# One Trainium2 core, a whole network: the seam between the two halves of its attention, and the routing of its experts, rearranged

## The chip, the cores and the metric

The kernel runs on one core of one Trainium2 chip. A core has five engines that run side by side, each from a queue of its own in fixed order: TensorE (PE) for matrix products, VectorE (DVE), ScalarE (ACT), GpSimd (POOL) and SyncE (SP), which mostly starts DMA transfers. They wait for each other through semaphores. The metric is the device time of one execution in microseconds; lower is better.

## The reference, cut to what matters

The reference is a chain of blocks over 512 tokens of width 1024: differential attention, a mixture of 16 experts, and then two layers of other mixers and feed-forward blocks. The change touches the first block and the routing of the second:

```
def diff_attention(x, w_in, ...):        # H = 8 heads, dh = 64
    q, k, v = split(x @ w_in)            # q, k: H x 2 x dh, normed over dh; v: H x 128
    for s in range(0, T, 128):           # 4 query blocks of 128, causal
        sc = q[s:s+128] . k[:s+128] - slope * distance
        p  = softmax(sc);  pd = p[first] - lam * p[second]
        outs.append(pd @ v[:s+128])
    return rmsnorm(concat(outs)) * (1 - lam0) @ w_out

def hier_moe(x, ...):                    # 4 groups of 4 experts
    logit_g = x @ w_group + b_group;   g_sel = argmax(logit_g)
    logit_e = (x @ w_router + b_router)[g_sel]
    top_v, top_i = top_k(softmax(logit_e), 2)
    # every token is computed by its two experts, weighted by top_v and the group's gate
```

## The kernel before

**Products.** Every large product is made three times with split operands (high part by high part, high by low, low by high): lines 139 to 141 where the tokens are the stationary side, 135 to 137 where the weights are. A weight block of 128x1024 numbers is split by a ScalarE cast (`wh`, L110) and a VectorE subtraction (`wl`, L111), so each block of weights costs both engines a step ahead of the products that read it (24 in a projection).

**Attention** is `stage_a`. Its eight heads are two halves, `G` = 0 and 1. `project(G)` makes q, k and v of a half: 48 units, 16 for each of q, k and v, each unit six products of 128x512. `headnorm` norms q and k per head: a VectorE sum (L445), the twelve small VectorE steps of `rsq` (L286 to L293), a scaling (L451), four TensorE transposes (L458) and a ScalarE copy (L459).

`attend(G)` is a list of 20 units. A unit holds the score products of a query block `i` and head `hh` (L487, two of them into the two banks named `s`), the transposes of an earlier head's probabilities (L505, into the only bank named `t`; ScalarE copies them out at L507), and the value products of a still earlier one (L514). Between the products VectorE adds the distances to the scores (L488) and mixes the two softmax parts (L494 to L497), and ScalarE takes the exponentials (L491). After the fourth head of a query block `onorm` norms the output (sum L526, `rsq`, scaling L530) and `turn_o` transposes it (L539) into the tiles `oh` and `ol`, which the output products `out(G)` read (8 units of 12 products, L135 to L137). For `i` = 0 a score product is 128x128, for `i` = 1 it is 128x256, then 384 and 512.

**Order.** `emit` writes units out in a given order, and `after(us, fn)` puts a step off by a number of units' cost. `weave(a, b)` merges two lists by the middle of each unit's cost, so that the units of the shorter list are spread evenly along the other; `tail=4` keeps the last four units of `b` for the end. The program before emits `project(0)`; then `attend(0)` woven with all 48 units of `project(1)`; then `attend(1)` woven with `out(0)`; then `out(1)`, whose results go through `route_step`.

**Routing.** For each of eight chunks `route_step` adds the residual (L378), squares it on ScalarE (L273) and adds the squares on GpSimd (L277), multiplies with the router's weights into the bank `lp` (L1171), transposes the chunk (L1177) and stores it to the buffer `xn` by a DMA that SP issues (L1180). `norm_r` sums the squares over partitions with eight products against ones (`ss`, L351), and `rsq` turns them into `rt`. `route` makes the logits `lg`, finds the best and the second expert in each group by two calls of `first_max`, forms the one-hot masks `M1`, `M2` and their sum `Mb`, and counts each token's place in its expert's list by products with a triangular matrix (`rk`, L1230). `rm` is that place (L1240, L1242). `places` compares it to a row of numbers (`oh`, L1300) and gets each expert's token numbers by products (`tk`, L1301) into `gix`. GpSimd then gathers those rows of `xn` into a tile `xe` (an indirect DMA, L1342), which has been cleared (L1322) because an expert's list is rarely full. `prep` transposes `xe` (L1353), and the first expert's products begin. `weigh` makes the tokens' weights, which GpSimd splits in three (L1288, L1291) for four small products each (`tkb`).

Of the kernel before, what the change touches and what calls it, by code (L numbers as in the profile page):

```python
# [29 lines left out]
def _constants():  # L30
# [26 lines left out]
    put("before", (p < j).astype(np.float32))  # L57
    put("iota", j)
    put("tokhi", np.broadcast_to((np.arange(NT)[:, None] * 128.0 - SKIP), (NT, 16)).reshape(1, -1))
# [22 lines left out]
class K:  # L82
# [261 lines left out]

    def norm_r(self, want_b=True, now=False):

        nc = self.nc
        ss = self.ptt("ss")
        for n, sq in enumerate((self.acc, self.acc2)):
            for i in range(NT):  # L350
                nc.tensor.matmul(ss[:, i:i + 1], lhsT=sq[:, i * P:(i + 1) * P], rhs=self.ones, start=n + i == 0, stop=n == 1,  # L351
                                 skip_group_check=True)
        self.rt = self.rsq(ss[:, :NT], NT, 1.0 / D, name="rt")
# [37 lines left out]
    def stage_a(self):  # L391
# [3 lines left out]
        with tc.tile_pool(name="pa", bufs=1) as pa:  # L395
# [76 lines left out]
            def attend(G):  # L472
                q, k, v = qkv[G]
                pvs, pt, p2s = {}, {}, {}

                def begin():
                    o[G] = (self.x8("oh"), self.x8("ol"))

                def score(i, hh):
# [40 lines left out]
                def onorm(i, pv):  # L520
# [12 lines left out]

                    def turn_o():
                        oh, ol = o[G]
                        qs = slice(i * P, i * P + P)
                        tp = self.ptt()
                        for hh in range(4):
                            nc.tensor.transpose(tp[:, hh * P:(hh + 1) * P], s[:, hh * P:(hh + 1) * P], self.ident)  # L539
                        tv = tp.rearrange("p (a b) -> p a b", a=4)  # L540
                        nc.scalar.activation(oh[:, :, qs], tv, AF.Copy, scale=gs[:, 1:2])
                        nc.vector.scalar_tensor_tensor(ol[:, :, qs], tv, gs[:, 1:2], oh[:, :, qs].bitcast(F32),
                                                       op0=OP.mult, op1=OP.subtract)
# [5 lines left out]
                for t in range(len(us) + ATT[1]):  # L549
# [8 lines left out]

                    def fn(parts=parts, t=t):
                        if t == 0:  # L560
                            begin()
                        for f, u, _ in parts:
                            f(*u)
# [8 lines left out]
            p1 = project(1)  # L572
            self.emit(self.weave(attend(0), p1))
            self.emit(self.weave(attend(1), out(0, self.add_h), tail=4))
            self.flush()
# [545 lines left out]
    def moe_begin(self, pool):  # L1121
# [14 lines left out]
        nc.scalar.dma_start(f, a["cst"][:, o:o + 388])  # L1136
        self.four = pr.tile([P, 4], F32, name="four")
        nc.gpsimd.tensor_copy(self.four, f[:, 0:4])
        nc.gpsimd.tensor_copy(self.before, f[:, 4:132])
# [14 lines left out]
    def route_step(self, pool):  # L1154
# [4 lines left out]
        def done(m, ps):  # L1159
# [8 lines left out]

            def turn():
                for i in range(NT):  # L1170
                    nc.tensor.matmul(self.lp[:, i * 20:(i + 1) * 20], lhsT=self.h[:, m, i * P:(i + 1) * P],  # L1171
                                     rhs=self.wrt[:, m], start=m == 0 and i == 0, stop=m == NK - 1, skip_group_check=True)
                if m == NK - 1:
                    self.norm_r(want_b=False)
                tp = self.ptt()
# [9 lines left out]
    def route(self):  # L1185
# [12 lines left out]
        parts(rt[:, :, None].to_broadcast([P, NT, NE]), 3)  # L1198
        fours = self.four[:, None, :].to_broadcast([P, NT * 5, 4])

        def first_max(src, tag):

            mx, eq, vm = (pr.tile([P, NT * 5, n], F32, name=tag + w) for w, n in (("m", 1), ("e", 4), ("v", 1)))
            nc.vector.tensor_reduce(mx, src, axis=AX.X, op=OP.max)
            nc.vector.tensor_tensor(eq, src, mx.to_broadcast([P, NT * 5, 4]), op=OP.is_equal)
            nc.vector.tensor_tensor(eq, eq, fours, op=OP.mult)
            nc.vector.tensor_reduce(vm, eq, axis=AX.X, op=OP.max)
            oh = pr.tile([P, NT, 5, 4], F32, name=tag + "o")
            nc.vector.tensor_tensor(oh.rearrange("p i g e -> p (i g) e"), eq, vm.to_broadcast([P, NT * 5, 4]),
                                    op=OP.is_equal)  # L1210
            return mx, oh


        lg4 = lg.rearrange("p i (g e) -> p (i g) e", e=4)
        mx, oh1 = first_max(lg4, "a")
        goh = oh1[:, :, 0, :, None].to_broadcast([P, NT, 4, 4])
        le2 = pr.tile([P, NT * 5, 4], F32, name="le2")
        nc.vector.scalar_tensor_tensor(le2, oh1.rearrange("p i g e -> p (i g) e"), NEG, lg4, op0=OP.mult, op1=OP.add)
        mx2, oh2 = first_max(le2, "b")
        M = [t3("M1", 4, 4), t3("M2", 4, 4)]  # L1220
# [11 lines left out]
        for j in range(NT):  # L1232
# [8 lines left out]
                                       op1=OP.mult)  # L1241
        nc.vector.tensor_scalar(rm, rm, -1.0, None, op0=OP.add)  # L1242

# [16 lines left out]
        def weigh():  # L1260

            lge, ges, dm, e2, w = t3("lge", 4), t3("ges", 1), t3("dm", 4), t3("e2", 1), t3("w", NE)
            mv = lambda t: t.rearrange("p (i g) o -> p i (g o)", g=5)
            nc.vector.tensor_tensor(lge, lg[:, :, 0:4], mv(mx)[:, :, 0:1].to_broadcast([P, NT, 4]), op=OP.subtract)
# [48 lines left out]
    def stage_b(self):  # L1313
# [5 lines left out]
        with tc.tile_pool(name="pb", bufs=1) as pb:  # L1319
            xes = [pb.tile([P, D], F32, name=f"xe{i}", tag=f"xe{i}") for i in range(3)]  # L1320
            for t in xes:
                nc.gpsimd.memset(t, 0.0)  # L1322
            flip = [0, 0]
# [401 lines left out]
```

## Time and profile before

| what | value |
|---|---|
| three timed runs | 1922.05, 1922.75, 1923.62 us |
| median | 1922.75 us |
| the profiled execution | 1921.22 us |
| its span | 1919.5 us |
| mean granted TensorE clock | 0.984 |
| TensorE busy | 1841.3 us, 96% |
| VectorE busy | 1321.3 us, 69% |
| ScalarE busy | 975.1 us |
| GpSimd busy | 227.3 us |

The profile is of one execution. Its span runs from the first instruction to the last; 1.7 us lie around it in that execution's time, which is 1.5 us under the median of the timed runs. The granted clock is 1.00 at 2.4 GHz and 0.50 at 1.2 GHz.

### The profile page before, as it was taken

To read this page: it belongs to the slowest core of one execution; us is meant where nothing else is said; L and a number is where in the kernel's file an instruction comes from. 1 tells how busy PE (TensorE), PEld (TensorE's weight loads), DVE (VectorE), ACT (ScalarE), POOL (GpSimd) and SP (SyncE) were. 2 spreads that over 40 slices of the span, in tenths; PEclk is the share of its full clock that TensorE was granted. 3 is DMA by queue.
4 is the path that set the end of the run, shared out by engine and by line. 5 is a ranking of instruction groups with operands and counts; after the bars stand their busy time and mean duration, and the time that the engine had idled before them with its cause. 6 is when DMAs were issued, how large, how long until landed. Compare 5 with 4: busy or idle time off the path is not lost.

```text
span 1919.5 us, 24632 instructions
## 1 busy us (share of the span) xinstructions
PE 1841.3 (96%) x8604; PEld 1451.1 (76%) x8605; DVE 1321.3 (69%) x2817; ACT 975.1 (51%) x1660; POOL 227.3 (12%) x281
## 2 busy tenths in 40 slices
PE   8999996999998999998999999999999999999997
PEld 6767585778887877675688888887877788888885
DVE  6586757999997779855677447744476677637753
ACT  5565554888885424436554224434276544324442
POOL 2000012222221301310200000012200100000001
PEclk9999897999999999999999999999999999999998
DMA  5521047999995454445233343334545233243331
GB/s 189 180 67 56 33 159 239 345 372 365 370 374 202 123 136 116 113 135 133 68 91 93 86 114 92 86 90 136 140 115 130 57 102 92 83 118 93 85 87 59
DMA packets 260098, 274.74 MB, mean 143 GB/s; under 512 B 14438, under 2 KB 175622, under 8 KB 259968
## 3 DMA queue, kind: packets, MB, share of 16 engines
q1 hardware_dynamic: 250688, 257.56, 43.8%
q0 software_dynamic: 5072, 10.00, 1.5%
q10 hardware_dynamic: 4208, 5.56, 0.8%
q8 instruction: 69, 1.13, 0.2%
q14 instruction: 61, 0.50, 0.1%
HBM read 238.19 MB, written 15.73 MB: 132 GB/s over the span
## 4 chain that ended last, share of the span: by engine, by line
PE 56%; DVE 7%; DMA 2%; ACT 2%; issue 1%; POOL 1%; SPq 0%; DVEq 0%; ACTq 0%; POOLq 0%
PE mm L135 15%; PE mm L137 15%; PE mm L136 15%; PE pv L721 2%; PE t L709 1%; DVE wl L111 1%; DVE sc L884 1%; DVE m L883 1%; PE mm L139 1%; PE mm L140 1%; PE mm L141 1%; PE s L694 1%; PE pv L1095 1%; DVE sb L697 1%; ACT sb L698 0%
## 5 line engine op out<-in xcount | busy, mean ns | idle before, releaser
L110 ACT CAST wh<-wr 128x1024 fp32r<-128x1024 f32 (+5 forms) x335 | 306.7, 916 | 440.6 <-PE mm L136 322.1
L111 DVE TENSOR_TENSOR wl<-wr,wh 128x1024 fp32r<-128x1024 f32 (+4 forms) x332 | 356.2, 1076 | 201.0 <-ACT wh L110 198.3
L135 PE MATMUL mm<-xh,wh 128*128 128x512 f32 x952 | 372.5, 391 | 2.0 <-DVE h L378 1.8
L137 PE MATMUL mm<-xh,wl 128*128 128x512 f32 x952 | 372.2, 391 | 0.2 <-DVE wl L111 0.2
L136 PE MATMUL mm<-xl,wh 128*128 128x512 f32 x952 | 371.3, 390 | 0.0
L135 PEld LDWEIGHTS mm<-xh,wh 128*128 128x128 f32 x952 | 178.8, 188 | 39.7 <-issue 3.5
L137 PEld LDWEIGHTS mm<-xh,wl 128*128 128x128 f32 x952 | 178.8, 188 | 37.9 <-issue 1.1
L136 PEld LDWEIGHTS mm<-xl,wh 128*128 128x128 f32 x952 | 178.8, 188 | 36.3 <-issue 0.2
L111 DVE TENSOR_TENSOR wl<-wx,wh 128x1024 fp32r<-128x1024 f32 x123 | 151.8, 1252 | 11.8 <-ACT wh L110 5.8
L110 ACT CAST wh<-wx 128x1024 fp32r<-128x1024 f32 x134 | 139.5, 1051 | 29.3 <-PE mm L141 24.4
L139 PE MATMUL mm<-wh,xh 128*128 128x512 f32 (+2 forms) x352 | 131.8, 378 | 9.7 <-ACT wh L110 5.6
L135 PE MATMUL mm<-hh,wh 128*128 128x512 f32 x352 | 138.9, 395 | 0.0
L136 PE MATMUL mm<-hl,wh 128*128 128x512 f32 x352 | 138.9, 395 | 0.0
L137 PE MATMUL mm<-hh,wl 128*128 128x512 f32 x352 | 138.9, 395 | 0.0
L140 PE MATMUL mm<-wl,xh 128*128 128x512 f32 (+2 forms) x352 | 130.0, 370 | 3.4 <-DVE wl L111 3.4
L141 PE MATMUL mm<-wh,xl 128*128 128x512 f32 (+2 forms) x352 | 129.0, 367 | 0.0
L618 DVE TENSOR_TENSOR z<-mm,rb 128x512 f32<-128x512 f32 x88 | 60.4, 688 | 81.0 <-PE mm L137 81.0
L139 PE MATMUL mm<-wh,xeh 128*128 128x512 f32 x256 | 103.8, 406 | 0.8 <-ACT xeh L1356 0.8
L277 POOL TENSOR_TENSOR acc<-acc,sq 128x512 f32<-128x512 f32 x42 | 58.1, 1383 | 387.6 <-ACT sq L273 387.2
L141 PE MATMUL mm<-wh,xel 128*128 128x512 f32 x256 | 101.6, 397 | 0.0
L140 PE MATMUL mm<-wl,xeh 128*128 128x512 f32 x256 | 101.2, 395 | 0.0
L378 DVE TENSOR_TENSOR h<-mm,h 128x512 f32<-128x512 f32 x88 | 60.5, 690 | 52.1 <-PE mm L137 50.9
(412 smaller groups left out, 3365.2 us busy)
## 6 DMA issues: line engine op xcount, KB each, us to landing
wr<-in_ffn_w_up SPq DMA_DIRECT2D x88, 512.0 KB, 4.9
wx<-in_moe_w_gate SPq DMA_DIRECT2D x23, 1024.0 KB, 9.4
wx<-in_moe_w_up SPq DMA_DIRECT2D x22, 1024.0 KB, 8.2
wx<-in_moe_w_down SPq DMA_DIRECT2D x22, 1024.0 KB, 9.9
wr<-in_ffn_w_down SPq DMA_DIRECT2D x32, 704.0 KB, 4.6
wr<-in_da_w_in SPq DMA_DIRECT2D x11, 1024.0 KB, 5.2
wr<-in_even_w_in SPq DMA_DIRECT2D x11, 1024.0 KB, 5.6
wr<-in_moe_w_up SPq DMA_DIRECT2D x10, 1024.0 KB, 8.4
```

The source lines that it names most:

```text
L110: nc.scalar.copy(h, raw)
L111: (nc.gpsimd if eng else nc.vector).tensor_tensor(l, raw, h.bitcast(F32), op=OP.subtract)
L135: mm(out, lhsT=wh, rhs=xh, start=first, stop=False, skip_group_check=True)
L136: mm(out, lhsT=wh, rhs=xl, start=False, stop=False, skip_group_check=True)
L137: mm(out, lhsT=wl, rhs=xh, start=False, stop=last, skip_group_check=True)
L139: mm(out, lhsT=xh, rhs=wh, start=first, stop=False, skip_group_check=True)
L140: mm(out, lhsT=xh, rhs=wl, start=False, stop=False, skip_group_check=True)
L141: mm(out, lhsT=xl, rhs=wh, start=False, stop=last, skip_group_check=True)
L277: nc.gpsimd.tensor_tensor(self.acc, self.acc, sq, op=OP.add)
L378: self.nc.vector.tensor_tensor(self.h[:, m], ps, self.h[:, m], op=OP.add)
L618: nc.vector.tensor_tensor(z[:, 2:], ps, self.rb, op=OP.mult)
L721: nc.tensor.matmul(pv[64 * e:64 * e + 64, j * P:], lhsT=heads[u]["v"](j), rhs=pt[:, 4 * j:3 * j + 4], start=j == 0, stop=j == NT - 1, skip ...
```

## The change

There are four edits.

1. `attend(0)` is woven with the first 40 units of `project(1)` only. The first four units of `attend(1)` (the scores of `i` = 0) are woven with the last eight units, which are value products; the other sixteen units of `attend(1)` go with `out(0)` as before. The tiles `oh` and `ol` are taken at the first use.
2. The products that sum the squares are in two parts, and in the routing they use a bank named `s` in place of `t`. The part that reads the running sum comes ahead of the last chunk's logits.
3. The best and second experts come from a comparison of each pair in a group: a logit's place is the number of logits ahead of it. The row of numbers counts from 1, which saves the subtraction of 1 from `rm`. What only the weights need moves into `weigh`.
4. ScalarE clears the three `xe` tiles, in place of GpSimd.

```
-    put("iota", j)
+    put("iota", j + 1)
...
+    def norm_sums(self, ss, n):
+
+        sq = (self.acc, self.acc2)[n]
+        for i in range(NT):
+            self.nc.tensor.matmul(ss[:, i:i + 1], lhsT=sq[:, i * P:(i + 1) * P], rhs=self.ones, start=n + i == 0, stop=n == 1,
+                                  skip_group_check=True)
...
                     def turn_o():
+                        if G not in o:
+                            o[G] = (self.x8("oh"), self.x8("ol"))
                         oh, ol = o[G]
...
             p1 = project(1)
-            self.emit(self.weave(attend(0), p1))
-            self.emit(self.weave(attend(1), out(0, self.add_h), tail=4))
+
+            self.emit(self.weave(attend(0), p1[:-8]))
+            a1 = attend(1)
+            self.emit(self.weave(a1[:4], p1[-8:]))
+            self.emit(self.weave(a1[4:], out(0, self.add_h), tail=4))
...
             def turn():
+                if m == NK - 1:
+                    ss = self.pst("ss")
+                    self.norm_sums(ss, 0)
                 for i in range(NT):
...
                 if m == NK - 1:
-                    self.norm_r(want_b=False)
+                    self.norm_r(want_b=False, ss=ss)
...
-        mx, oh1 = first_max(lg4, "a")
+        vs = pr.tile([P, NT * 5, 4, 4], F32, name="vs")
+        own = lambda j, n: lg4[:, :, j:j + 1].to_broadcast([P, NT * 5, n])
+        nc.vector.tensor_tensor(vs, lg4[:, :, None, :].to_broadcast([P, NT * 5, 4, 4]),
+                                lg4[:, :, :, None].to_broadcast([P, NT * 5, 4, 4]), op=OP.is_gt)
+        for j in range(1, 4):
+            nc.vector.tensor_tensor(vs[:, :, j, 0:j], lg4[:, :, 0:j], own(j, j), op=OP.is_ge)
+        place = pr.tile([P, NT * 5, 4], F32, name="place")
+        nc.vector.tensor_reduce(place, vs, axis=AX.X, op=OP.add)
+        oh1, oh2 = (pr.tile([P, NT, 5, 4], F32, name=n) for n in ("oh1", "oh2"))
+        for n, oh in enumerate((oh1, oh2)):
+            nc.vector.tensor_scalar(oh.rearrange("p i g e -> p (i g) e"), place, float(n), None, op0=OP.is_equal)
...
-        mx2, oh2 = first_max(le2, "b")
...
-        nc.vector.tensor_scalar(rm, rm, -1.0, None, op0=OP.add)
...
-                nc.gpsimd.memset(t, 0.0)
+                nc.scalar.activation(t, self.ones.to_broadcast([P, D]), AF.Copy, scale=0.0)
```

The instructions of each engine stand in one fixed order, before and after. On TensorE, at the end of `project(1)` (products of L139 to L141) and the start of `attend(1)` (`s` scores, `t` transposes, `pv` value products, `mm<-oh,wh` and the like the output products), the rows before are these; the left name is what an instruction writes.

```order
L141 MATMUL mm<-wh,xl_110 128x512
L487 MATMUL s<-kt,qt 128x128 x7
L505 MATMUL t<-ident,p_1962 128x128
L514 MATMUL pv<-v,pt 128x128
L539 MATMUL t<-ident,os 128x128 x4
L487 MATMUL s<-kt,qt 128x128
L487 MATMUL s<-kt,qt 128x256
L135 MATMUL mm<-oh,wh 128x512 x2
```

In the change the same place reads as follows, from one pair of scores to the last projection product and the first output product.

```order
L490 MATMUL s<-kt,qt 128x128 x2
L508 MATMUL t<-ident,p_1982 128x128
L139 MATMUL mm<-wh,xh_108 128x512
L140 MATMUL mm<-wl,xh_108 128x512
L141 MATMUL mm<-wh,xl_110 128x512
L139 MATMUL mm<-wh,xh_108 128x512
L140 MATMUL mm<-wl,xh_108 128x512
L141 MATMUL mm<-wh,xl_110 128x512
L490 MATMUL s<-kt,qt 128x256 x2
L517 MATMUL pv<-v,pt 128x128 x2
...
L135 MATMUL mm<-oh,wh 128x512
```

The four pairs of 128x128 scores have moved among the last 48 projection products (this is the last of the four pairs), and the first 128x256 score stands right behind the last of these products. From the last score of `attend(0)` to the end of the projection there were 66 products and are now 102; the last 42 of them stand among the pairs.

On VectorE, between the logits and the mask `Mb` (`am`, `bm` are the group maxima, `ae` to `ao` and `be` to `bo` the steps of `first_max`), before has these rows among others:

```order
L1196 TENSOR_TENSOR lg<-lg,rows 128x80
L1204 TENSOR_REDUCE am<-lg 128x20
L1205 TENSOR_TENSOR ae<-lg,am 128x80
...
L1209 TENSOR_TENSOR ao<-ae,av 128x80
L1218 SCALAR_TENSOR_TENSOR le_2968<-ao,lg 128x80
...
L1204 TENSOR_REDUCE bm<-le_2968 128x20
...
L1209 TENSOR_TENSOR bo<-be,bv 128x80
...
L1225 TENSOR_TENSOR Mb<-M_2979,M_2980 128x64
```

The change has there:

```order
L1203 TENSOR_TENSOR lg<-lg,rows 128x80
L1210 TENSOR_TENSOR vs<-lg 128x320
L1263 TENSOR_REDUCE mx<-lg 128x20
L1213 TENSOR_TENSOR vs<-lg 128x20
L1213 TENSOR_TENSOR vs<-lg 128x20x2
L1213 TENSOR_TENSOR vs<-lg 128x20x3
L1269 TENSOR_TENSOR lge<-lg,mx 128x16
L1215 TENSOR_REDUCE place<-vs 128x80
L1275 TENSOR_REDUCE ges<-lge 128x4
L1218 TENSOR_SCALAR oh_2964<-place 128x80
L1218 TENSOR_SCALAR oh_2965<-place 128x80
...
L1225 TENSOR_TENSOR Mb<-M_2968,M_2969 128x64
```

From the second `lg` to `Mb` there were 19 instructions between; there are 13.

On ScalarE, behind the last stores' copies (`xk`) and the first exponential of `weigh` (`lge`), the change has these rows, where before the second exponential came next and then two casts:

```order
L1186 COPY xk<-t 128x512 x2
L1273 ACTIVATE lge<-lge 128x16
L1327 ACTIVATE xe_3046<-ones 128x1024
L1327 ACTIVATE xe_3047<-ones 128x1024
L1327 ACTIVATE xe_3048<-ones 128x1024
L110 CAST wh<-wx 128x1024
L1274 ACTIVATE e_3061<-e_3061 128x4
L110 CAST wh<-wx 128x1024
L1361 CAST xeh<-t 128x512 x2
```

The three clears stand ahead of the first cast and of the second exponential, which two small chains (the weights, and the first expert's low parts) wait for.

## Rows read from the trace of the kernel before

**Rows 1.** The page: busy times, and the granted clock in 40 slices.
```profile
PE 1841.3 (96%) x8604; PEld 1451.1 (76%) x8605; DVE 1321.3 (69%) x2817; ACT 975.1 (51%) x1660; POOL 227.3 (12%) x281
...
PEclk9999897999999999999999999999999999999998
```

**Rows 2.** Three stretches: length, busy of PE, PEld, DVE, ACT, POOL, clock, DMA.
```profile
188.66:194.10 5.44, 3.73 (x22) 2.61 (x21) 5.39 (x42) 3.60 (x13) 0.00 (x0) 1.00 0.82 255
194.10:207.00 12.90, 12.90 (x33) 7.37 (x32) 6.56 (x34) 5.56 (x19) 0.00 (x0) 0.50 0.14 56
207.00:211.03 4.03, 3.93 (x18) 2.19 (x18) 2.88 (x18) 2.12 (x7) 0.00 (x0) 0.91 0.00 0
```

**Rows 3.** Timeline of PE: start, duration, instruction, idle before it and its releaser.
```profile
188.12 0.39 PE L140 MATMUL mm<-wl,xh 128*128 128x512 f32 x1
188.34 0.39 PE L141 MATMUL mm<-wh,xl 128*128 128x512 f32 x1
188.66 0.49 PE L487 MATMUL s<-kt,qt 64*128 64x128 f32 x4
189.63 2.24 PE L487 MATMUL s<-kt,qt 64*128 64x128 f32 x10 [0.47 <-DVE st L488]
...
211.03 0.92 PE L487 MATMUL s<-kt,qt 64*128 64x384 f32 x4
```

**Rows 4.** Two stretches of 10 us, columns as in group 2.
```profile
160.00:170.00 10.00, 8.32 (x41) 5.57 (x40) 8.62 (x32) 4.72 (x11) 0.00 (x0) 1.00 0.33 107
...
210.00:220.00 10.00, 9.78 (x44) 5.29 (x43) 8.88 (x50) 6.77 (x21) 0.00 (x0) 1.00 0.00 0
```

**Rows 5.** PE's longest wait between 80 and 188 us.
```profile
PE t L458 <- ACT pt L507: 1.7, 1, 1.7
```

**Rows 6.** Timeline of DVE: first and last row of the k norms' bunch.
```profile
151.56 0.68 DVE L445 TENSOR_REDUCE qss<-sq 128x8 f32<-128x512 f32 x1
...
163.86 1.21 DVE L111 TENSOR_TENSOR wl<-wr,wh 128x1024 fp32r<-128x1024 f32 x1
```

**Rows 7.** Timeline of all engines, routing, 291 to 300 us.
```profile
291.32 1.02 PE L351 MATMUL ss<-ones,acc 128*128 128x1 f32 x8 [0.60 <-ACT xk L1179]
...
295.95 0.24 DVE L1196 TENSOR_TENSOR lg<-lg,rows 128x80 f32<-128x80 f32 x1
...
299.60 0.22 DVE L1225 TENSOR_TENSOR Mb<-M,M 128x64 bf16<-128x64 f32 x1
```

**Rows 8.** Timeline of all engines, routing, 300 to 313 us.
```profile
300.27 1.99 ACT L110 CAST wh<-wx 128x1024 fp32r<-128x1024 f32 x2 [0.92 <-DMA xn<-xk]
...
300.38 2.89 POOL L1322 MEMSET xe<- 128x1024 f32 x3 [2.32 <-DMA xn<-xk]
...
300.53 0.22 DVE L1240 SCALAR_TENSOR_TENSOR rm<-rk,Ms 128x64 f32<-128x64 f32 x1
...
300.79 0.60 DVE L1242 TENSOR_SCALAR rm<-rm 128x64 f32<-128x64 f32 x1
...
301.42 1.98 DVE L1300 TENSOR_SCALAR oh<-iota,rm 128x128 bf16<-128x128 bf16 x6
...
303.84 0.15 DVE L1307 TENSOR_SCALAR gix<-tf 128x1 int32<-128x1 f32 x1
...
304.88 1.25 POOL L1342 DMA_INDIRECT xe<-xn,gix  x1 [1.61 <-DVE w L1279]
...
309.71 0.88 PE L1353 MATMUL t<-ident,xe 128*128 128x128 f32 x3 [5.18 <-DVE ohl L1432]
...
311.28 0.41 DVE L1300 TENSOR_SCALAR oh<-iota,rm 128x128 bf16<-128x128 bf16 x2
...
312.09 0.78 PE L139 MATMUL mm<-wh,xeh 128*128 128x512 f32 x1
```

**Rows 9.** A stretch in the experts' products, columns as in group 2.
```profile
360.00:420.00 60.00, 60.00 (x290) 48.03 (x289) 59.75 (x82) 50.80 (x60) 18.37 (x11) 1.00 1.03 372
```

**Rows 10.** SP's longest waits there and ahead, 314 to 584 us.
```profile
SPq L1333 <- DVE wl L111: 93.6, 42, 4.7
```

More of the change, by code (lines that the diff above doesn't have):

```diff
@@ L343, in new_acc, with norm_r @@
         self.acc = self.sm.tile([P, T], F32, name="acc", tag="sq", bufs=3)
-    def norm_r(self, want_b=True, now=False):
-        nc = self.nc
[L348 to L352, printed above, removed]
+    def norm_sums(self, ss, n):
[3 more added lines that the diff above has]
+                                  skip_group_check=True)
+    def norm_r(self, want_b=True, now=False, ss=None):
+        nc = self.nc
+        if ss is None:
+            ss = self.ptt("ss")
+            self.norm_sums(ss, 0)
+        self.norm_sums(ss, 1)
         self.rt = self.rsq(ss[:, :NT], NT, 1.0 / D, name="rt")
@@ L474, in attend @@
                 pvs, pt, p2s = {}, {}, {}
-                def begin():
-                    o[G] = (self.x8("oh"), self.x8("ol"))
                 def score(i, hh):
@@ L557, in attend, with fn @@
                     cost = sum(c * (u[0] + 1) * 0.45 for _, u, c in parts)
-                    def fn(parts=parts, t=t):
-                        if t == 0:
-                            begin()
+                    def fn(parts=parts):
                         for f, u, _ in parts:
@@ L1136, in moe_begin @@
         nc.scalar.dma_start(f, a["cst"][:, o:o + 388])
-        self.four = pr.tile([P, 4], F32, name="four")
-        nc.gpsimd.tensor_copy(self.four, f[:, 0:4])
         nc.gpsimd.tensor_copy(self.before, f[:, 4:132])
@@ L1169, in turn @@
             def turn():
+                if m == NK - 1:
+                    ss = self.pst("ss")
+                    self.norm_sums(ss, 0)
                 for i in range(NT):
@@ L1198, in route @@
         parts(rt[:, :, None].to_broadcast([P, NT, NE]), 3)
[L1199 to L1211, printed above, removed]
-        lg4 = lg.rearrange("p i (g e) -> p (i g) e", e=4)
-        mx, oh1 = first_max(lg4, "a")
+        lg4 = lg.rearrange("p i (g e) -> p (i g) e", e=4)
+        vs = pr.tile([P, NT * 5, 4, 4], F32, name="vs")
[9 more added lines that the diff above has]
+            nc.vector.tensor_scalar(oh.rearrange("p i g e -> p (i g) e"), place, float(n), None, op0=OP.is_equal)
         goh = oh1[:, :, 0, :, None].to_broadcast([P, NT, 4, 4])
-        le2 = pr.tile([P, NT * 5, 4], F32, name="le2")
-        nc.vector.scalar_tensor_tensor(le2, oh1.rearrange("p i g e -> p (i g) e"), NEG, lg4, op0=OP.mult, op1=OP.add)
-        mx2, oh2 = first_max(le2, "b")
         M = [t3("M1", 4, 4), t3("M2", 4, 4)]
@@ L1262, in weigh @@
             lge, ges, dm, e2, w = t3("lge", 4), t3("ges", 1), t3("dm", 4), t3("e2", 1), t3("w", NE)
+            mx = pr.tile([P, NT * 5, 1], F32, name="mx")
+            nc.vector.tensor_reduce(mx, lg4, axis=AX.X, op=OP.max)
+            le2 = pr.tile([P, NT * 5, 4], F32, name="le2")
+            nc.vector.scalar_tensor_tensor(le2, oh1.rearrange("p i g e -> p (i g) e"), NEG, lg4, op0=OP.mult, op1=OP.add)
+            mx2 = pr.tile([P, NT * 5, 1], F32, name="mx2")
+            nc.vector.tensor_reduce(mx2, le2, axis=AX.X, op=OP.max)
             mv = lambda t: t.rearrange("p (i g) o -> p i (g o)", g=5)
```

## Prediction

> **What bounds the kernel now.** I began with the page [rows 1]: TensorE is busy for 96% of the span and its clock is 1.00 almost everywhere, so an edit gains only where TensorE stands idle or runs at the lower clock. The slices show such places; those that the change touches I looked at in short stretches and in the timeline.
>
> The first is the seam of the two attention halves [rows 2, 3]. The last projection product starts at 188.34 us. Then TensorE has only small scores to do: in 5.44 us its records add up to 3.73 and VectorE's to 5.39, and the idle time is released by the distance sum (L488). So VectorE is the limit there, and TensorE's supply is thin. Behind that the granted clock is 0.50 for 12.90 us, with TensorE busy all the time and VectorE for only 6.56. Then it rises to 0.91. From the end of the projection (188.6) to the first score of `i` = 2 (211.0) pass 22.4 us.
>
> What would that work need at 2.4 GHz? The 22 small instructions of the first stretch are worth less than their records, since each waits for VectorE on its own: four back to back take 0.49, so 22 take 2.7 us. The second stretch is 12.90 x 0.50 = 6.45, the third 3.93 x 0.91 = 3.6.
>
> The second place is the routing [rows 7, 8]. From 291.3 to 312.1 TensorE waits for a chain of small VectorE steps and then for the gather (5.18 us in the last wait alone). Each step saved on that chain brings the first expert product (312.09) forward.
>
> What is won there is kept: in the experts' products TensorE is busy 60.00 of 60 us [rows 9], the DMA engines too, but the transfers wait for buffers that VectorE frees (93.6 us in 42 waits [rows 10]), so they move with the engines.
>
> **The seam (edit 1).** (a) The `i` = 0 scores go among the last 48 projection products. They cost TensorE their 2.7 us there. Products start 0.22 to 0.23 us apart [rows 3], so 48 take 10.8 and the place becomes 13.5 us long. VectorE must do in it what it did in 5.39 us, two weight splits (1.21 each [rows 6]), and the last norm of the first half, some 3 to 4 us: 11 to 12 of 13.5. It fits, barely. I put 0.5 us of waiting; ends 0 and 2.
>
> (b) Behind the last projection product now comes the `i` = 1 part: 6.45 + 3.6 us of TensorE, plus one output product more in front of the first `i` = 2 score (the order has 15 for 14), 10.3. VectorE has 6.56 + 2.88 = 9.4. The two are close; a stretch of a like mix at full clock, 210 to 220, has TensorE at 9.78 and VectorE at 8.88 of 10 [rows 4]. So I take 10.8. That supposes the clock stays up, because no stretch is left in which TensorE has only small scores; the rival prices the other case. Gain: 22.4 - 2.7 - 0.5 - 10.8 = 8.4 us.
>
> (c) The first half's weave loses 48 of 288 products, so its VectorE work lies beside 10.8 us less of TensorE's. Where is VectorE late? In the bunch of the k norms at the end: 65 rows from 151.56 to 163.86 take 12.3 us [rows 6], and TensorE idles 1.68 us of the ten that follow (8.32 busy [rows 4]), nearly all in one wait of a transpose, 1.7 us [rows 5]. In the change's order VectorE has 58 rows between the sum for the last pair of `attend(0)`'s scores and the weight split that a product needs next. At the pace of the bunch that is 58/65 x 12.3 = 11.0 us. TensorE has 30 products (6.8) and, by the order, 17 small ones (at 0.12 to 0.2 some 2.4) meanwhile, 9.2. It waits 1.8 us for that split; I take 1.6 on top of what it waits now. Ends: -1.7 (today's wait goes) and +5 (VectorE's lag adds up over the weave). The edit's sum is 8.4 - 1.6 = **6.8**, between 3 and 10.
>
> **The sum of squares (edit 2).** The eight products wait 0.60 us at 291.32 [rows 7]. In the change the first four need only GpSimd's sum, finished before the last chunk is added, and the bank `s`, and the others stand right behind the logits. The products themselves stay on the path, so I take **0.6**; ends 0 and 1. If GpSimd were late, the last logits would queue behind that wait.
>
> **The places (edit 3).** From the second `lg` (295.95) to `Mb` (299.60) pass 3.65 us over 20 starts, 0.18 each [rows 7]. The change has 14 starts, 2.6 us, one of them with 320 elements. The trace has no such comparison: 80 elements take 0.24 [rows 7], 512 take 0.68 [rows 6], which puts 320 at 0.48, so 0.25 more. Gain **0.8**; ends 0 (broadcast comparisons cost double) and 1.2. The wait of `ges` for ScalarE's exponential stands in front of the one-hots as before, and the clears come behind that exponential. Leaving out L1242 saves from its start to the next, 300.79 to 301.42 [rows 8]: **0.6**.
>
> The six one-hots ahead of the first `gix` take 1.98 us, 0.33 each, while GpSimd clears tiles (2.89 from 300.38); two later ones take 0.41, 0.20 each [rows 8]. L1242 itself takes 0.60 at 64 elements, beside 0.22 for the step before it. If GpSimd's clearing is what stretches them, its removal gives 6 x 0.13 = **0.8**; end 0. The Trainium skill has a rule for it, in "SBUF — State Buffer", section "Who interferes with whom": VectorE's copies, casts and scalar operations in their two-port modes share a port pair with GpSimd, whoever is first blocks the other, and ScalarE waits for no one. By that rule the 0.8 counts whole and ScalarE's clears do not bring it back; by a trace reading without it the routing's sum below is 0.8 smaller.
>
> **The clears (edit 4).** Two ScalarE casts of 128x1024 take 1.99 us [rows 8], so three clears take 3.0. They wait, as GpSimd's did until 300.38, for the last stores of `xn`, which now leave 0.6 us earlier. So they run from about 299.7 to 302.7, the first until 300.7; the first gather would issue at 304.88 - 2.8 = 302.1 and needs only the first. 1.4 us are to spare; without them the clears would cost what they are late by. Behind the clears the two casts end at 304.7, far ahead of the first product. The second exponential is late by 3 us, and `w` and GpSimd's split behind it; `tkb` now stands behind six expert products, 2.6 us at 0.43 apiece. I cost it at nothing; end 1 us. Gather to first transpose (304.88 to 309.71, 4.8 us) and from there to the first product (2.4) I leave as they are; with eight transposes in a row the latter may lose 0.5.
>
> Routing: 0.6 + 0.8 + 0.6 + 0.8 = **2.8**, between 1 and 4.5.
>
> **Sum.** 6.8 + 2.8 = 9.6 us off 1921.22, the profiled execution's own time: 1911.6. That execution lies 1.5 under the median of the runs, so the median goes from 1922.75 to 1913.1.
>
> **Rivals.**
>
> *VectorE takes more back.* The first half's weave and the last 48 products are both near VectorE's limit [rows 4, 6]: stalls of 4 us in (c) and 2 in (a) in place of 1.6 and 0.5 leave 9.6 - 3.9 = 5.7: 1917. For it speaks that TensorE already waits once there; against it that before the bunch it has spare time.
>
> *The clock falls all the same.* Behind the projection VectorE and TensorE are nearly level, and a few waits of TensorE in the first `i` = 1 units could look like 188 to 194, where busy 3.73 of 5.44 came ahead of the fall [rows 2]. As long a stretch at 0.50 costs 6.45: gain 3.1, 1919.6. Against it: at 210 to 220 the clock is 1.00 with the same engines close to level [rows 4]. The Trainium skill, in "TensorE: Matmul & The Clock Gate", section "HAM oscillation — how this bites in real kernels", tells of kernels whose short work between waits lets the clock drop each time; by it the seam before is such a place, and after would be one only if TensorE's waits there came back.
>
> *Nothing that can be measured.* The 8.4 is taken up where the work went (five more in (c), two in (a)) and the gather's start does not follow `gix` (it came 1.0 us after it [rows 8], beside another VectorE step): about 2 us left, 1921.
>
> *Slower.* One mechanism: the weight split in (c) is late enough for TensorE's busy share to fall as it did at 188 to 194. Then the 48 products behind it run at half clock, 10.8 us more, and the wait itself takes 5: 9.6 - 10.8 - 5 + 1.6 = -4.6, 1927.4. [...] Against it: 1.68 us idle in 160 to 170 left the clock at 1.00 [rows 4].
>
> **How the numbers follow.** Forecast 0.62, VectorE takes more 0.17, clock 0.09, nothing 0.06, slower 0.06. This measurement can tell about 0.2%, 3.85 us, so faster is below 1918.9: the first two cases and a little of the third, 0.81; same 0.13; slower 0.06. The forecast's own ends are 1922.75 - 14.5 = 1908.2 and 1922.75 - 4 = 1918.7; taking in the clock's case, the range is 1908 to 1919.6.
>
> **What would show it.** The seam: clock 1.00 from the last projection product on, the first `i` = 2 score some 11 us behind it in place of 22.4, and a wait of 3 us for a weight split near the k norms. The routing: `ss` without its wait, `Mb` 2.8 us behind the second `lg`, one-hots of 0.2, the gather 2.8 us earlier against the last output product. I am wrong if the clock is at 0.50 anywhere ahead of 211 us, if TensorE's idle time before the last projection product grows by over 5 us, or if the gather waits for the clears.

## The result, and the profile after

The changed kernel takes 1910.43 us (1909.12 to 1911.44), against 1922.4 for the kernel before (the median of four runs, 1919.91 to 1923.62): a ratio of 0.9937, 95% interval 0.9923 to 0.995, so 12.1 us less (9.6 to 14.8). The forecast was 1913.1 and faster. The profiled execution has a span of 1908.9 us, 10.6 less than before.

The page of the changed kernel, busy times and the granted clock in 40 slices, beside [rows 1]:

```profile
PE 1835.4 (96%) x8604; PEld 1448.6 (76%) x8605; DVE 1318.4 (69%) x2815; ACT 978.0 (51%) x1663; POOL 226.3 (12%) x277
...
PEclk9999998999999999999999999999999999999998
```

The dent of the clock in the fifth slice is gone. The stretches of the changed kernel (length, busy of PE, PEld, DVE, ACT, POOL, clock, DMA) run from the first score of the first half to the last projection product, from there to the first score of `i` = 2, and from there to the last output product; behind them are the start and end rows of the middle one in TensorE's timeline, which answer to [rows 2, 3]:

```profile
85.30:194.19 108.89, 106.49 (x539) 75.75 (x539) 82.93 (x384) 65.33 (x149) 0.00 (x0) 1.00 0.18 59
194.19:204.26 10.07, 9.85 (x48) 5.58 (x47) 8.45 (x42) 6.88 (x22) 0.00 (x0) 1.00 0.30 104
204.26:279.76 75.50, 75.18 (x400) 57.45 (x399) 51.73 (x174) 44.60 (x92) 8.19 (x6) 1.00 0.36 116
```

```profile
194.19 0.39 PE L141 MATMUL mm<-wh,xl 128*128 128x512 f32 x1
194.51 0.70 PE L490 MATMUL s<-kt,qt 64*128 64x256 f32 x4
...
204.26 0.92 PE L490 MATMUL s<-kt,qt 64*128 64x384 f32 x4
```

The same first stretch of the kernel before:

```profile
83.82:188.34 104.52, 101.83 (x516) 73.62 (x516) 76.60 (x333) 60.91 (x131) 0.00 (x0) 1.00 0.19 61
```

So the first stretch grew by 4.37 us, the seam went from 22.69 (188.34 to 211.03 in [rows 3]) to 10.07 at full clock, and the third stretch, which took 77.22 before, lost 1.72, of which one output product (about 0.23) has only moved ahead of the cut. From the first score to the last output product the changed kernel needs 9.97 us less.

The routing in the changed kernel's timeline, all engines, beside [rows 7, 8]:

```profile
281.26 0.95 PE L349 MATMUL ss<-ones,acc 128*128 128x1 f32 x8
...
282.97 1.03 PE L349 MATMUL ss<-ones,sq 128*128 128x1 f32 x8
...
286.69 0.24 DVE L1203 TENSOR_TENSOR lg<-lg,rows 128x80 f32<-128x80 f32 x1
...
288.26 2.95 ACT L1327 ACTIVATE xe<-ones 128x1024 f32<-128x1024 f32 x3
...
289.29 0.30 DVE L1225 TENSOR_TENSOR Mb<-M,M 128x64 bf16<-128x64 f32 x1
...
289.65 0.30 DVE L1237 TENSOR_SCALAR tokv<-M 128x64 bf16<-128x64 f32 x1
...
290.46 1.07 DVE L1305 TENSOR_SCALAR oh<-iota,rm 128x128 bf16<-128x128 bf16 x6
...
291.73 0.15 DVE L1312 TENSOR_SCALAR gix<-tf 128x1 int32<-128x1 f32 x1
...
292.77 1.25 POOL L1347 DMA_INDIRECT xe<-xn,gix  x1 [3.25 <-DVE e L1272]
...
294.30 1.57 SPq L1338 DMA_DIRECT2D wx<-in_moe_w_gate  x2
...
297.50 1.94 PE L1358 MATMUL t<-ident,xe 128*128 128x128 f32 x8 [5.09 <-DMA xe<-xn,gix]
...
299.26 0.79 PE L139 MATMUL mm<-wh,xeh 128*128 128x512 f32 x1
```

The steps of the two timelines side by side (us):

| step | before | after | gain | forecast |
|---|---|---|---|---|
| last output product to second `lg` | 7.70 | 6.93 | 0.77 | 0.6 |
| to `Mb` | 3.65 | 2.60 | 1.05 | 0.8 |
| to `rm` (L1240) | 0.93 | 0.91 | 0.02 | 0 |
| to the first one-hot | 0.89 | 0.26 | 0.63 | 0.6 |
| to `gix` | 2.42 | 1.27 | 1.15 | 0.8 |
| to the gather's start | 1.04 | 1.04 | 0 | 0 |
| to the first transpose | 4.83 | 4.73 | 0.10 | 0 |
| to the first expert product | 2.38 | 1.76 | 0.62 | 0 |
| together | 23.84 | 19.50 | 4.34 | 2.8 |

Of the 4.34, 1.41 is given back up to the first expert's hidden transposes, which follow the first product by 22.05 us before and 23.46 after: six products start early, but at the lower clock, about 0.43 us apart, and TensorE then waits 0.40 for GpSimd's split. Net 2.93. The 22.05 is of one execution; in e10_before_again the same instructions have 22.78 there, but 23.13 in place of 23.84 ahead of it, so the net is the same.

The profiled executions also differ where the change does not touch them. The first score of the first half comes 1.48 us later in the changed kernel's, whose clock was at 0.83 in 20 to 30 us (1.00 before). From the first expert's hidden transposes to the end it takes 0.86 us more: its clock has a dent in 664 to 689 us that the other lacks (mean 0.93 there, 1.00 before), some 1.75 us, and part of that comes back elsewhere. 9.97 + 2.93 - 1.48 - 0.86 = 10.6, the difference of the spans, where the medians differ by 12.

### The profile page after: what moved, and what is told of

Read it like the earlier page. It is cut to its first block, busy times and chain, and to the rows that moved or that the text cites. A ratio compares the mean times of both kernels' runs of the same rounds, so it can differ in the third digit from the quotient of the medians.

```text
span 1908.9 us, 24634 instructions
## 1 busy us (share of the span) xinstructions
PE 1835.4 (96%) x8604; PEld 1448.6 (76%) x8605; DVE 1318.4 (69%) x2815; ACT 978.0 (51%) x1663; POOL 226.3 (12%) x277
## 3 DMA queue, kind: packets, MB, share of 16 engines
q8 instruction: 69, 1.13, 0.2%
## 4 chain that ended last, share of the span: by engine, by line
PE 51%; DVE 2%; ACT 2%; DMA 1%; POOL 1%; SPq 1%; issue 1%; DVEq 0%; POOLq 0%; ACTq 0%
PE mm L137 14%; PE mm L135 14%; PE mm L136 14%; PE pv L727 2%; PE t L715 1%; PE s L700 1%; PE pv L1101 1%; PE mm L140 1%; PE mm L139 1%; PE mm L141 1%; DMA rsw<-qd 0%; SPq L391 0%; POOL rsw L392 0%; PE s L1067 0%; PE t L1086 0%
## 5 line engine op out<-in xcount | busy, mean ns | idle before, releaser
L111 DVE TENSOR_TENSOR wl<-wr,wh 128x1024 fp32r<-128x1024 f32 (+4 forms) x332 | 356.8, 1078 | 196.4 <-ACT wh L110 193.7
L111 DVE TENSOR_TENSOR wl<-wx,wh 128x1024 fp32r<-128x1024 f32 x123 | 151.3, 1247 | 11.7 <-ACT wh L110 5.6
L139 PE MATMUL mm<-wh,xh 128*128 128x512 f32 (+2 forms) x352 | 132.0, 380 | 9.7 <-ACT wh L110 5.6
L141 PE MATMUL mm<-wh,xl 128*128 128x512 f32 (+2 forms) x352 | 129.7, 369 | 0.0
L139 PE MATMUL mm<-wh,xeh 128*128 128x512 f32 x256 | 103.9, 406 | 0.8 <-ACT xeh L1361 0.8
L141 PE MATMUL mm<-wh,xel 128*128 128x512 f32 x256 | 101.8, 398 | 0.0
```

Of the source, the lines that this page charges most:

```text
L111: (nc.gpsimd if eng else nc.vector).tensor_tensor(l, raw, h.bitcast(F32), op=OP.subtract)
L139: mm(out, lhsT=xh, rhs=wh, start=first, stop=False, skip_group_check=True)
L141: mm(out, lhsT=xl, rhs=wh, start=False, stop=last, skip_group_check=True)
```

## The experiments

**e1_seam**: the kernel before with the first edit alone.

```
-            self.emit(self.weave(attend(0), p1))
-            self.emit(self.weave(attend(1), out(0, self.add_h), tail=4))
+            self.emit(self.weave(attend(0), p1[:-8]))
+            a1 = attend(1)
+            self.emit(self.weave(a1[:4], p1[-8:]))
+            self.emit(self.weave(a1[4:], out(0, self.add_h), tail=4))
```

> The kernel before with the first edit alone (the weave of the attention halves). Theory: the seam gives most of the gain, by filling the lull of TensorE and so keeping its clock at 2.4 GHz: 6.8 us by the prediction, 8 to 9 by the changed kernel's trace, which reaches the first score of query block 2 6.8 us earlier although its clock rose 1.5 us late at the start, and the last output product 8.5 us earlier. So 1913 to 1916 us, ratio about 0.996, and the 10 us after the last projection product at clock 1.00. Rival: the gain is the routing's and the seam's is taken back by VectorE in the thinner weave: within 3 us of before.

1913.4 us, ratio 0.9955 (0.9938 to 0.9971): 8.7 us less. The three stretches are 108.85, 10.05 and 75.52 us, those of the changed kernel. The theory held; the rival fell. The profiled execution of e1_seam gives some of it back behind the seam: from the last output product to the first expert's hidden transposes it takes 48.93 us, where the kernel before has 45.89 and, in e10_before_again, 45.91. TensorE's clock was at 0.51 in its first 5 us of expert products (0.85 and 0.67 in the other two) and at 0.84 in the 10.6 us ahead of those transposes (1.00 in the other two). Whether the edit brings that on or chance did was not tried.

**e2_routing**: the changed kernel with the one weave of before (the lines above turned round).

> The changed kernel with the weave of before, so the three routing edits alone. Theory: from the last output product to the first expert product 23.8 us become 19.5, as in the changed kernel's trace, of which 1.5 us are lost again behind it; the kernel gains 2.8 to 4.3 us, 1918 to 1920. Rival: the stretch is shorter but the experts' products start with their buffers no earlier, so all of it is lost by the end of the experts: no change of the whole.

1918.19 us, ratio 0.9978 (0.9965 to 0.9992): 4.2 us less. The routing takes 19.51 us and 23.35 behind it. 8.7 and 4.2 add up to 12.9, against 12.1 for both; the intervals allow that the parts simply add.

**e10_before_again**: the kernel before once more.

> The kernel before, a second profile. Theory: the seam's cost hangs on when the clock falls and rises, and that varies between executions of the same instructions (in the run with ScalarE's clears alone the stretch from the last projection product to the first score of query block 2 took 18.98 us in place of 22.69, and nothing was changed there). So 18 to 23 us here, while the routing, in which TensorE hardly works, repeats within 0.2 us: 23.8. Rival: the 18.98 came from the other buffers of that kernel, and here it is 22.7 again within 0.2.

The seam took 18.82 us, with not an instruction changed. Its windows (columns as above):

```profile
188.44:194.00 5.56, 4.15 (x19) 2.70 (x18) 5.18 (x40) 3.91 (x14) 0.00 (x0) 0.77 0.67 239
194.00:198.00 4.00, 4.00 (x15) 2.46 (x13) 2.71 (x17) 1.92 (x7) 0.00 (x0) 0.50 0.52 195
198.00:207.26 9.26, 9.16 (x41) 5.28 (x39) 6.79 (x38) 5.77 (x20) 0.00 (x0) 0.98 0.00 0
```

The clock fell inside the lull, in place of behind it, and was back some 9 us sooner than in [rows 2]. Six executions had the old seam: 22.69 and 22.66 (e2), and 18.82, 18.98 (e3), 18.08 (e8) and 18.85 (e9). The new seam took 10.05 to 10.07 in four (e1, the changed kernel, e4, e11), all at clock 1.00. So the theory held: the clock fell in all six executions with the lull, for a time that changed from one to the next, and the rival of other buffers fell, since here not an instruction was changed. The routing took 23.13, not 23.8 within 0.2: GpSimd's clears came at another moment, and other steps of VectorE met them. That part of the expectation was wrong.

**e3_clears**: the kernel before with ScalarE's clears alone (in e4_pool_clears and e11_pool_clears_again the line is turned back in the changed kernel).

```
-                nc.gpsimd.memset(t, 0.0)
+                nc.scalar.activation(t, self.ones.to_broadcast([P, D]), AF.Copy, scale=0.0)
```

> The kernel before with the clears on ScalarE alone. Theory of contention: GpSimd's clears stretch VectorE's scalar operations; the six one-hots take some 1.1 us in place of 1.98, the subtraction of 1 some 0.2 in place of 0.60, and the first product comes 1.0 to 1.4 us earlier, measured from the last output product. Rival: these operations are slow for another reason (the write of 16-bit numbers, their place in the queue): their times stay within 0.2 us.

The timeline of VectorE in e3_clears, against L1242 and L1300 in [rows 8]:

```profile
296.94 0.22 DVE L1242 TENSOR_SCALAR rm<-rm 128x64 f32<-128x64 f32 x1
297.21 1.05 DVE L1300 TENSOR_SCALAR oh<-iota,rm 128x128 bf16<-128x128 bf16 x6
```

0.22 in place of 0.60 and 1.05 in place of 1.98. The routing took 21.49 us, 2.35 less than in [rows 7, 8] and 1.64 less than in e10_before_again, more than expected either way.

**e4_pool_clears and e11_pool_clears_again**: the changed kernel with GpSimd's clears, twice.

> The changed kernel with the clears back on GpSimd. Theory of contention: the six one-hots take about 1.9 us again in place of 1.07 and the gather starts about 0.8 us later. Rival as in the run before: 1.1 us stays, and the gather waits for the clears only if these end behind gix, which the trace would show as a wait of GpSimd on itself.

> The changed kernel with GpSimd's clears, a second profile. Theory: the block repeats, since the clears begin when the stores of the normed rows have landed and VectorE's first scalar operation behind that waits to their end: the step that writes the third column of the token numbers takes 2 to 2.5 us, and the gather lands 2 us later after its start than in the changed kernel (7.1 us in place of 4.7), because two loads of weights are issued while it still makes its descriptors. From the last output product to the first expert product 23.8 us again. Rival: both were chance of one execution, and this one shows 20 to 22 us.

The routing took 23.83 and 24.39 us: with GpSimd's clears the other routing edits gain nothing up to the first product. The one-hots took 1.07 both times, so the place that I had named was wrong, and the gather started 1.97 us later, not 0.8. The timeline of e11_pool_clears_again shows the block on another step:

```profile
287.49 2.75 POOL L1327 MEMSET xe<- 128x1024 f32 x3
...
287.94 2.47 DVE L1237 TENSOR_SCALAR tokv<-M 128x64 bf16<-128x64 f32 x1
...
292.59 1.21 DVE L111 TENSOR_TENSOR wl<-wx,wh 128x1024 fp32r<-128x1024 f32 x1
...
293.12 1.80 POOL L1347 DMA_INDIRECT xe<-xn,gix  x1 [2.57 <-DVE dm L1271]
293.82 1.92 SPq L1338 DMA_DIRECT2D wx<-in_moe_w_gate  x2
...
300.77 0.45 PE L1358 MATMUL t<-ident,xe 128*128 128x128 f32 x1 [8.01 <-DMA xe<-xn,gix]
```

L1237 takes 2.47 us in place of 0.30 and ends with the last clear. And the first transpose of the gathered rows comes 7.65 us after the gather's start (7.09 in e4_pool_clears, 4.73 in the changed kernel): there the first of two loads of weights is issued 0.70 us after the gather starts, while GpSimd is still busy with it for 1.80; in the changed kernel it is issued 1.53 after it, behind its 1.25.

These kernels differ from the changed one in more than the clears. The order of VectorE's instructions has changed too: a weight split (L111 above, at 292.59) stands ahead of the second `gix`, where the changed kernel has a short step, `ohl` (L1437, 0.27 us). So of the 4.3 and 4.9 us only 1.98, between `Mb` and `rm`, are the block by the clears; 2.4 and 2.9 are the later transpose, which goes with the earlier loads, and what brings it was not tried by itself.

The times, 1911.63 and 1912.14 in one run each, are only 1 to 2 us above the changed kernel's, but the loss is in them. The first expert's hidden transposes come 46.54 and 46.99 us behind the last output product, against 42.95. The spans differ by no more than 1.0 and 1.5 us because the changed kernel's profiled execution reached its first score 1.6 to 1.7 us later and took 0.8 to 1.0 us more behind those transposes, where the instructions do not differ.

**e8_places and e9_sums**: the kernel before with the third edit alone, and with the second alone.

> The kernel before with the third edit alone: pair comparisons, numbers from 1, the weights' maxima later; GpSimd clears as before. Theory of contention: the chain from the second logits step to the mask shortens from 3.65 to 2.6 us, as in the changed kernel, but the clears then meet other scalar operations of VectorE, which wait for them: from the last output product to the first expert product 22.5 to 24 us in place of 23.8, so at most a third of the 1.7 us that the shorter chain and the missing subtraction are worth. Rival: the edits add up, 22.1 us.

22.64 us from the last output product to the first expert product: 0.5 less than in e10_before_again and 1.2 less than in [rows 7, 8], inside the range of the theory. But 1.2 is more than the third of the 1.7 that it allowed, and the rival's 22.1 is 0.5 away, so it stands only in that some is lost. `lg` to `Mb` is 2.60; the time goes back in the step on `tokv` (L1228 there, 1.13 in place of 0.30) and in the one-hots (1.61).

> The kernel before with the second edit alone, the sums of squares in two parts. Theory: the second logits step comes 0.6 to 0.8 us earlier against the last output product (7.70 before); the rest of the routing waits for GpSimd's clears, which begin when the last stores have landed, so less than half of it reaches the first expert product (23.84 before). Rival: it reaches it whole, 23.1.

24.66 us, worse than both forecasts. The second `lg` does come 0.77 earlier. But the timeline shows

```profile
293.36 1.23 DVE L111 TENSOR_TENSOR wl<-wx,wh 128x1024 fp32r<-128x1024 f32 x1
294.50 0.31 DVE L1234 TENSOR_TENSOR Mb<-M,M 128x64 bf16<-128x64 f32 x1
294.62 2.04 SPq L1342 DMA_DIRECT2D wx<-in_moe_w_gate  x2
...
298.98 1.25 POOL L1351 DMA_INDIRECT xe<-xn,gix  x1 [4.24 <-DVE e L1284]
```

a weight split of the experts now stands ahead of `Mb` in VectorE's queue, which makes `lg` to `Mb` 4.89 us, and frees buffers, so that the first of the weights' loads goes out 4.4 us ahead of the gather, whose first transpose comes 6.59 after its start.

**e5_scores_first, e6_last4, e7_last16**: the changed kernel with other weaves.

```
-            self.emit(self.weave(a1[:4], p1[-8:]))
+            self.emit(a1[:4] + p1[-8:])                  # e5
+            self.emit(self.weave(a1[:4], p1[-4:]))       # e6, with p1[:-4] beside attend(0)
+            self.emit(self.weave(a1[:4], p1[-16:]))      # e7, with p1[:-16] beside attend(0)
```

> The changed kernel with the four units of the second half's first scores written ahead of the last eight projection units, not woven with them. TensorE has the same instructions as in the changed kernel. Theory: what counts is that VectorE's work on these scores has products beside it; here the first three pairs come nearly back to back, TensorE waits for the distance sums there, some 2 to 4 us, the clock may fall among the 48 products behind (by a busy share as in 188 to 194 us of before) and they would then cost up to 6 us more. 1912 to 1919 us; the stretch from the first score of the first half to the last projection product is 2 to 9 us longer than 108.9. Rival: it is enough that the projection's products stand behind the scores at all, and the weave does not matter: 108.9 us within 1, and the time of the changed kernel.

1912.62 us, ratio 0.996 (0.9948 to 0.9971); first stretch, seam and third stretch:

```profile
85.24:194.78 109.54, 107.19 (x539) 76.54 (x539) 82.62 (x388) 65.82 (x150) 0.00 (x0) 1.00 0.18 58
194.78:204.35 9.57, 9.36 (x45) 5.34 (x43) 7.49 (x38) 6.14 (x20) 0.00 (x0) 1.00 0.36 110
204.35:281.94 77.59, 77.16 (x403) 58.26 (x402) 51.99 (x175) 44.97 (x93) 8.21 (x6) 1.00 0.35 113
```

The theory fell, the rival's stretch held: up to the seam the weave does not matter, as long as projection products stand behind the scores. The rival's time is doubtful: the interval just meets the changed kernel's, and the third stretch is 77.59 in place of 75.50, with 0.3 us of waits. Of these 2.09 us 0.50 are work that the cut moves: 14 output products stand ahead of the first `i` = 2 score in place of 15. VectorE is less busy in the third stretch's first 30 us (26.56 in place of 28.31); why that order feeds it later was not tried. The step from the last output product to the second `lg` took 7.58 us here and 7.40 in e6_last4, in place of 6.93, with the same routing; the cause of that is open too.

> The changed kernel with the first four units of the second half woven with the last four projection units in place of eight, and 44 units beside the first half. Theory: the thinner weave of the first half costs little (in the changed kernel TensorE's idle time in it did not grow), so a thicker one gives nothing back; the four units have 24 products, 5.4 us, for VectorE's 5 to 6 us, so TensorE waits 1 to 2 us there. The stretch from the first score to the last projection product 108 to 110.5 us; the whole within 2 us of the changed kernel. Rival: VectorE's lag in the thinner weave costs, and with four units it is shorter by 1 to 2 us.

1908.73 us, ratio 0.9944 (0.9924 to 0.9965); 109.54 us. As expected, not to be told from the changed kernel, though TensorE's one long wait there, 1.5 us, was for ScalarE's copy (L510), not for VectorE.

> The changed kernel with the first four units of the second half woven with the last sixteen projection units, so 32 units beside the first half. Theory: the first half's weave loses 22 us of products against before, more than VectorE can spare at the norms of k, and TensorE waits 2 to 6 us more there; behind it the four units have more cover than they need. The stretch from the first score to the last projection product is 111 to 115 us in place of 108.9, the whole 1912 to 1917 us. Rival: VectorE has time enough all over the weave: 108.9 within 1.

1915.57 us, ratio 0.9969 (0.9955 to 0.9982); 112.64 us, as expected. TensorE's waits up to there:

```profile
PE t L544 <- DVE os L533: 1.3, 2, 0.7
PE t L544 <- DVE rsqt L292: 1.1, 1, 1.1
PE t L544 <- DVE rsq L293: 1.0, 1, 1.0
PE t L508 <- ACT pt L510: 0.6, 1, 0.6
```

Here VectorE's lag in a thinner weave is real: TensorE waits 3.4 us for it, where in the changed kernel it waits 1.6.

## Why the prediction was right, point by point

**The seam** was forecast at 6.8 us and gave 8.7 alone in the timed runs (5.6 to 11.9). That the lull drops the clock, and that filling it keeps the clock, was right: the stretch at 0.50 of [rows 2] is gone, and the second rival with it. How much that is worth is less certain than either number: from the first score of the first half to the last output product the new seam's executions take 194.4 to 194.5 us, 10.0 less than the 204.43 on which I built, but 5.2 to 6.3 less than the four executions with a shorter old seam (199.68 to 200.75). That the forecast of 6.8 lies near the 8.7 is thus in part luck. Its terms:

- (b) 22.4 to 10.8: both count from the first score behind the projection, and so counted after is 9.75 (194.51 to 204.26), 1 us better than forecast. But the 22.4 was one execution. In four of six the old seam took 18.1 to 19.0, so the trace on which I built had a long one, and the term is 3.7 to 4.6 us smaller where the clock rises sooner. This is the mis-sized step. It is part of why the times of kernels with the old seam spread over 8 to 10 us (before 1916.15 to 1925.38 and 1916.95 to 1926.89, e2_routing 1913.14 to 1921.64) and those with the new one over 2 to 5 (the changed kernel 2.3, e1_seam 3.05, e5_scores_first 4.7): the seam's own six values lie within 4.6 us.
- (a) and (c) together 2.7 + 0.5 + 1.6 = 4.8, measured 4.37, but by another way. TensorE's busy time grew by 4.66 and its idle time fell from 2.69 to 2.40. The trace has 23 more rows there, so each moved one cost about 0.20 us among products, more than 0.12 back to back. The waits for VectorE grew from 0.6 to 1.6 us, but those for ScalarE fell from 2.1 to 0.6, the 1.7 of [rows 5] among them. The wait for a weight split is 0.7 us:

```profile
PE mm L140 <- DVE wl L111: 0.7, 1, 0.7
PE t L544 <- DVE os L533: 0.7, 2, 0.4
PE t L508 <- ACT pt L510: 0.6, 1, 0.6
PE s L490 <- DVE st L491: 0.2, 1, 0.2
```

  So my 1.8 us at the k norms was wrong; e7_last16 shows that the limit lies one step further.
- The third stretch's 1.72 us I had not forecast. It comes with the edit (75.47 to 75.52 wherever the changed kernel's weave stands, 77.20 to 77.25 with the old one), but e5_scores_first and e7_last16, which share the list that comes behind, have 77.59. One output product of it has moved ahead of the cut, as (b) had counted, and 0.60 is idle time of TensorE (0.92 before, 0.32 after); the cause of the rest in the order stays open.

**The routing**: 2.8 forecast, 2.9 net in the trace, 4.2 in the timed runs (1.5 to 6.7). The table has the steps. The sums, the chain and L1242 were sized well. That GpSimd's clears hold VectorE's scalar steps was right, and it is shown: 2.47 us for a step of 0.30. In the kernel before, the three clears and the six one-hots of [rows 8] fall into parts:

```profile
301.27 1.00 POOL L1322 MEMSET xe<- 128x1024 f32 x1
302.22 1.06 POOL L1322 MEMSET xe<- 128x1024 f32 x1
...
301.42 0.97 DVE L1300 TENSOR_SCALAR oh<-iota,rm 128x128 bf16<-128x128 bf16 x3
302.31 1.09 DVE L1300 TENSOR_SCALAR oh<-iota,rm 128x128 bf16<-128x128 bf16 x3
```

Three one-hots end 0.12 us behind the second clear, at 302.27, and three 0.12 behind the third, at 303.28. The rule from "SBUF — State Buffer", section "Who interferes with whom" in the Trainium skill agrees: a blocked step ends with a clear, to 0.2 us. What was wrong is to price it as a term of its own on the one-hots. It falls on whichever scalar step meets the clears, so it eats part of what the other edits bring: second and third edit alone gave -0.8 and +1.2 us against [rows 7, 8], the clears alone 2.35, all three 4.33 (each 0.7 less against e10_before_again). In e9_sums no scalar step met a clear; there the longer way to `Mb` (4.89 us) and the later transpose (6.59) took the gain.

The clears on ScalarE started 8.5 us behind the last output product (288.26), right behind the exponential and without a wait for a store, not 11.4 as forecast. The last copy for the stores came 1.65 us sooner there (4.77 us behind the last output product in place of 6.42), not 0.6. So 3.45 us were to spare, from the first clear's end at 289.32 to the gather, not 1.4.

**The rivals.** VectorE took back less than was priced (1.0 us more of waits up to the seam, and 1.5 less for ScalarE), the clock did not fall (1.00 from 85 to 280 us), and the cases of nothing and of slower were far off. Of the signs, `ss` without its wait, `Mb` 2.6 us behind the second `lg` and one-hots of 0.2 came, and the gather came 3.6 us earlier in place of 2.8; the wait of 3 us for a weight split did not come (0.7). The clock was low ahead of 211 us only in the first 30 us, before the change begins, where it was low in the kernel before too; by its words alone that sign of being wrong came true.

## What to carry to other kernels

A lull in front of dense TensorE work is worth more than its idle time, and a place where the clock falls has a cost that changes from one execution to the next: before sizing a gain from one profile, look at the same stretch in a second one. Fill such a lull with small work moved beside products that are there anyway, until the engine that runs beside them is full. And do not add the gains of steps on one chain where another engine can block the chain's next step: move that engine's work first, then shorten the chain, and look again at the order of the queues, which changes with it.

## What the runs showed of the hardware that was not expected

- The same instructions of the old seam ran 12.90 us at 0.50 in one execution [rows 2], and in another 4.0 us fully at 0.50 with parts at 0.77 and 0.98 beside it (18.82 us in place of 22.69).
- A VectorE scalar operation that came 0.45 us after the start of three GpSimd clears waited to the end of all three (2.47 us in place of 0.30, in e4_pool_clears and e11_pool_clears_again alike). Elsewhere one clear's end was enough: in the kernel before L1242 ended at 301.38, behind the first clear's 301.33, and in e8_places the step on `tokv` (L1228 there), which began with the first clear, ended 0.16 us behind it. What decides between the two was not tried.
- The first transpose of the gathered rows came 4.65 to 4.83 us after the gather's start in the ten executions where the first of the two next loads of weights (`w_gate`) was issued at least 1.4 us behind that start, and 6.59 to 7.65 in the three where it was issued earlier. In the ten, too, another load (`w_down`) had gone out 2.8 to 4.9 us ahead of the gather. That the loads cause it was not tried by itself.
